# Bias lines drawn in fp32 at the start of an encoder kernel, with their operands loaded on ScalarE's queue

## The chip, the cores and the metric

The kernel runs on one core of one Trainium2 chip. The metric is the device time of one execution in microseconds. Before the change it is 1682.21 us, the median of three runs from 1681.28 to 1682.70 us.

## What is computed

One encoder layer with 1024 channels is run over 1024 sample rows and 256 prompt rows. Every row is normalised (RMS norm with a gain), multiplied with a wide input matrix to queries, keys, values and gates, goes through a windowed attention branch with sinks and a dilated attention branch, is merged by gates, and passes a squared-ReLU MLP. What matters here is the bias table: 32 buckets by 20 heads, looked up by relative position and added to the attention logits.

```python
rel = np.arange(3 * n)[None, :] - n - np.arange(n)[:, None]
bias = bias_table.astype(jnp.float32)[_rel_bucket(rel * dist_scale)]
...
logits = jnp.where(valid[None, :, None, None], s + bias, NEG_INF)
```

## The kernel before

The kernel computes nearly everything on TensorE (PE) with numbers that are split in two parts, hi and lo, each of the type fp32r, and three matmuls for each product. The splitting is done on ScalarE (ACT, the hi part) and VectorE (DVE, the lo part). Each engine works off its instructions strictly in the order in which the program is written; the code around the change fixes that order by hand.

**The opening.** The ten row tiles of 128 rows are loaded by SP's queue (load_x, L684 to L686), with the gain gm (L810) and the value columns of the input matrix (load_v, L688 to L696) between them. For each tile, `square` (L733) takes the row's sum of squares and its root on ACT, `scale` (L740) multiplies by the reciprocal and the gain on DVE and so makes xn, and `turn` (L748) transposes xn on PE (eight 128x128 transposes, L338) and splits the result from PSUM (hi on ACT, L769, lo on DVE, L771). `split_v` (L698) splits the value weights. `values` (L792) then multiplies: 24 matmuls of 128x512 for each tile, L798. Fillers on PE are issued by `warm` (L708): matmuls of the identity by itself, 15 ahead of the first tile, 4 behind the first tile's transposes, 2 behind the second's. The order written out at L831 to L887 is: square, scale and transposes of tile 0, warm(4), square and scale of tile 1, the split of tile 0, transposes of tile 1, warm(2), and then the value matmuls.

**The bias lines.** The bias depends on the relative position alone, so the kernel draws 2048 positions ("lines", NL = 2048) for all 20 heads: a one-hot matrix of 33 rows (32 buckets, and one row for masked positions with -1e30) by 2048 positions, an input made on the host, is multiplied by the table. Before the change this is done in four steps of 512 positions, one in each of the tiles 3 to 6 (`draw`, L722): the table is split into tab_hi and tab_lo on DVE (L861, L862), POOL loads 512 columns of the one-hot rows (`load_hot`, L715, tile hs) and converts them to fp32r (L720, tile hr), PE makes two matmuls (L727), ACT copies 20x512 out of PSUM (L729), and POOL stores them in the DRAM scratch scr_l (L730). From the first pair of column blocks on, `line` (L296) spreads scr_l for the attention.

**Loads and their counters.** SP and ACT each have a hardware queue for loads and stores. The framework gives these transfers eight completion counters, DMAHW0 to DMAHW7, in turn, in the order in which the program writes the transfers, whichever of the two queues they are on. A transfer that takes over a counter is preceded, on the engine that issues it, by a wait until the counter's last user has landed. POOL's transfers have counters of their own (DMASW).

Of the kernel before, what the change touches and what calls it, by code (L numbers as in the profile page):

```python
# [10 lines left out]
F32 = mybir.dt.float32  # L11
F32R = mybir.dt.float32r
AF = mybir.ActivationFunctionType
ALU = mybir.AluOpType

P = 128
D = 1024
# [6 lines left out]
AH = 8  # L24
BH = 4
FF = 4 * D
EPS = 1e-6
NEG = -1e30
BUCKETS, MAXD = 32, 1024
# [68 lines left out]
def encoder_kernel(  # L98
# [5 lines left out]
    nc = tc.nc  # L104
# [15 lines left out]
    const = ctx.enter_context(tc.tile_pool(name="const", bufs=1))  # L120
# [6 lines left out]
    def slot(name, shape=(P, D), dt=F32):  # L127
        return slots.tile(list(shape), dt, name=name, tag="m", bufs=N_M)
# [7 lines left out]
    def bank(tag, name=None):  # L136
        return psum.tile([P, 512], F32, name=name or tag, tag=tag, bufs={"mm": 3, "sc": 2, "pt": 2, "pv": 1}[tag])
# [111 lines left out]
    nc.vector.memset(eps, EPS)  # L249
    bg = const.tile([P, 2 * KC], F32, name="bg")  # L250
    nsink = const.tile([P, AH], F32, name="nsink")
    tab = const.tile([BUCKETS + 1, AH + 3 * BH], F32, name="tab")
    tab_hi, tab_lo = (const.tile([BUCKETS + 1, AH + 3 * BH], F32R, name=x) for x in ("tab_hi", "tab_lo"))

    nm_b = const.tile([P, ROWS], F32, name="nm_b")
    l_b = const.tile([P, ROWS], F32, name="l_b")
# [19 lines left out]
    NH = AH + 3 * BH  # L276
# [16 lines left out]
    NL = sum(x[5] for x in LINES)  # L293
    scr_l = dram.tile([NH, NL], F32, name="scr_l")
# [378 lines left out]
    with ExitStack() as pre:  # L673
        late = pre.enter_context(tc.tile_pool(name="values", bufs=1))

        def own(name, shape, dt=F32, n=1):
            return late.tile(list(shape), dt, name=name, tag=name, bufs=n)
# [6 lines left out]
        def load_x(t):  # L684
            xs[t] = slot("xt")
            nc.sync.dma_start(xs[t], x_rows(t))  # L686
# [11 lines left out]
        def split_v(v, i, eng=nc.vector):  # L698
            if v == 0:
                hi, lo = wslot("vhi", (P, 2, 512), F32R), wslot("vlo", (P, 2, 512), F32R)  # L700
            else:
                hi, lo = own("v2", (P, 2, 384), F32R, 8), own("v2", (P, 2, 384), F32R, 8)
            src = v_raw.pop((v, i))
            nc.scalar.activation(hi, src, AF.Copy)
            eng.tensor_tensor(lo, src, hi.bitcast(F32), op=ALU.subtract)
            v_parts[v, i] = hi, lo

        def warm(n):  # L708
            ps = bank("mm", "warm")
            for _ in range(n):  # L710
                nc.tensor.matmul(ps[:, :P], ident, ident, start=True, stop=True, skip_group_check=True)

        hots = {}

        def load_hot(i):  # L715
            if i < NL // 512:
                hs = own("hs", (P, 512))[: BUCKETS + 1, :]
                nc.gpsimd.dma_start(hs, hot[:, 512 * i : 512 * i + 512])
                hots[i] = own("hr", (P, 512), F32R)[: BUCKETS + 1, :]
                nc.gpsimd.tensor_copy(hots[i], hs)  # L720

        def draw(i):  # L722

            ps = bank("pv", "line")
            hs = hots.pop(i)
            for k, x in enumerate((tab_lo, tab_hi)):
                nc.tensor.matmul(ps[:NH, :], x, hs, start=not k, stop=k == 1)  # L727
            ln = own("vo", (P, 512), n=2)[:NH, :]
            nc.scalar.activation(ln, ps[:NH, :], AF.Copy)  # L729
            nc.gpsimd.dma_start(scr_l[:, 512 * i : 512 * i + 512], ln)  # L730
            load_hot(i + 1)

        def square(t):  # L733
            xn[t] = slot("xn")
            ss = small.tile([P, 1], F32, name="ss")
            nc.scalar.activation(xn[t], xs[t], AF.Square, accum_out=ss)
            sds[t] = small.tile([P, 1], F32, name="sd")
            nc.scalar.activation(sds[t], ss, AF.Sqrt, bias=eps, scale=1.0 / D)

        def scale(t):  # L740
            rs = small.tile([P, 1], F32, name="rs")
            nc.vector.reciprocal(rs, sds.pop(t))
            nc.vector.scalar_tensor_tensor(xn[t], xs.pop(t), rs, gm, op0=ALU.mult, op1=ALU.mult)
# [48 lines left out]
        def values(t, v, ps, ks=range(KC)):  # L792
            n = NV[v]
            for k in ks:
                lh, ll = h_at(k, P * t, P)
                rh, rl = (x[:, k % 2, :] for x in v_parts[v, k // 2])
                for j, (a, b) in enumerate(((lh, rh), (lh, rl), (ll, rh))):
                    nc.tensor.matmul(ps[:, :n], a, b, start=k == 0 and j == 0, stop=k == KC - 1 and j == 2)  # L798

        def evac(t, v, ps):  # L800
            rows = slice(P * t, P * t + P)
            vo = own("vo", (P, 512), n=2)[:, : NV[v]]
            if v == 0:
                nc.vector.tensor_copy(vo, ps)
            else:
                nc.scalar.activation(vo, ps[:, : NV[v]], AF.Copy)
            nc.gpsimd.dma_start(scr_v[rows, 512 * v : 512 * v + NV[v]], vo)
# [5 lines left out]
            load_v(0, i)  # L813
        for t in range(2, 6):
            load_x(t)
        nc.sync.dma_start(tab[:BUCKETS, :], rel_bias)
        nc.sync.dma_start(bg, b_gate[0].rearrange("(k p) -> p k", p=P))
        nc.sync.dma_start(nsink, sink[0].partition_broadcast(P))
        load_v(1, 0)
# [10 lines left out]

        turns = [turn(t) for t in range(NT)]  # L831
        square(0)
        scale(0)
        next(turns[0])
        warm(4)
        square(1)
        scale(1)
        next(turns[0])
        split_v(0, 0)
        next(turns[1])  # L840
        warm(2)
        split_v(0, 1)
        next(turns[1])
        split_v(0, 2, nc.gpsimd)
# [12 lines left out]
        next(turns[1], None)  # L857
        square(4)
        next(turns[2], None)
        nc.vector.memset(tab[BUCKETS:, :], NEG)  # L860
        nc.vector.tensor_copy(tab_hi, tab)  # L861
        nc.vector.tensor_tensor(tab_lo, tab, tab_hi.bitcast(F32), op=ALU.subtract)  # L862
        load_hot(0)
        nc.vector.tensor_scalar(nsink, nsink, -1.0, None, op0=ALU.mult)
        for t in range(2):
            evac(t, 0, pss[t])
# [2 lines left out]
        for t in range(2, NT):  # L869
            if t + 1 < NT:  # L870
                next(turns[t + 1])
                next(turns[t + 1])
            if t + 3 < NT:
                square(t + 3)
            if t + 2 < NT:
                scale(t + 2)
            if t + 1 < NT:
                next(turns[t + 1], None)
            if t < 6:
                split_v(1, t - 2)  # L880
            if t > 7:
                next(b0)
            ps = bank("mm", "v")
            values(t, 0, ps)
            if 3 <= t < 3 + NL // 512:
                draw(t - 3)
            evac(t, 0, ps)  # L887

        def more():
# [14 lines left out]
        for t in (4, 5, 6, 7, 8, 9, 0, 1, 2, 3):  # L904
            ps = bank("mm", "v")
# [6 lines left out]
    if True:  # L912
# [16 lines left out]
        class Rows:  # L929
# [15 lines left out]
            def sum(self, t0, n, ps, other):  # L945
                out, a, b = self.views(t0, n, ps, other)
                nc.vector.scalar_tensor_tensor(out, a, self.scale, b, op0=ALU.mult, op1=ALU.add)
# [401 lines left out]
    if True:  # L1349
# [54 lines left out]
        n = len(order)  # L1404
# [87 lines left out]
        for i, (x, b, c) in enumerate(jobs):  # L1492
            t0, n = BLOCKS[b]
# [15 lines left out]
            ps = bank("mm")  # L1509
# [79 lines left out]
    with ExitStack() as pre:  # L1589
# [20 lines left out]
        for hh in range(2):  # L1610
# [17 lines left out]
            for t in range(NT):  # L1628
                m = parts.pop(t)
                ps = bank("mm")  # L1630
# [391 lines left out]
```

## Time and profile before

| | |
|---|---|
| median of three runs | 1682.21 us |
| the profiled execution's own time | 1681.33 us |
| its span, first to last instruction | 1679.5 us |
| busy PE, DVE, ACT, POOL | 1667.2, 951.4, 718.2, 512.1 us |
| mean granted TensorE clock | 0.999 |

A row of the timeline gives the start in us, the duration in us, the engine, the line, the operation, what is written from what, and in brackets the idle time before it and what ended it. "SPq" and "ACTq" are transfers as the engine issues them. An fp32 matmul that isn't fp32r has two records in the trace (15 fillers have 30). The rows of transfers give the size and the time from the issue to the landing.

### The profile page before, as it was taken

Reading aid. Unit: us, or ns where it says so; the run is one execution under the profiler, and the core shown is the slowest. Engines: PE = TensorE matmul, PEld = TensorE weight load, DVE = VectorE, ACT = ScalarE, POOL = GpSimd, SP = SyncE. Lnnn points to the kernel's source line nnn. Section 1 sums busy time; section 2 is a strip of 40 time slices with the busy share of each in tenths; the row PEclk is TensorE's granted clock in tenths of the full one; section 3 lists DMA queues with packets and bytes.
Section 4 is the critical chain, followed back from the end, with each engine's and each line's share of the span. In section 5 each row is a group of like instructions: output and inputs, shape, how many; then the busy total and the mean of one; then the engine's idle time right before and its main releaser. Section 6 shows DMA issues by size and latency. Waiting matters only on the chain. (4 is left out here: it accounts for less than half of the span.)

```text
span 1679.5 us, 24942 instructions
## 1 busy us (share of the span) xinstructions
PE 1667.2 (99%) x9268; PEld 1414.5 (84%) x9268; DVE 951.4 (57%) x1544; ACT 718.2 (43%) x1485; POOL 512.1 (30%) x404
## 2 busy tenths in 40 slices
PE   9999999999999999999999999999999999999998
PEld 7898888887788888888888888888888888888886
DVE  6732233455563566677278445545556775867665
ACT  6332323356662556654176333333334333333445
POOL 1312222122111463200100556556454250514240
PEclk9999999999999999999999999999999999999999
DMA  7426562567676793845121443443356934733333
GB/s 249 151 58 127 133 133 76 162 192 197 192 198 188 184 262 119 296 133 201 38 88 59 160 156 109 136 160 115 125 190 227 363 105 131 256 102 116 120 119 125
DMA packets 225881, 262.45 MB, mean 156 GB/s; under 512 B 30017, under 2 KB 154737, under 8 KB 225761
## 3 DMA queue, kind: packets, MB, share of 16 engines
q1 hardware_dynamic: 217536, 239.80, 44.8%
q0 software_dynamic: 7936, 20.54, 5.6%
q8 instruction: 73, 1.20, 0.3%
q10 hardware_dynamic: 288, 0.52, 0.1%
q14 instruction: 48, 0.39, 0.1%
HBM read 175.13 MB, written 90.92 MB: 158 GB/s over the span
## 5 line engine op out<-in xcount | busy, mean ns | idle before, releaser
L347 PE MATMUL dn<-dhi,ulo 128*128 128x512 f32 x448 | 174.5, 389 | 0.2
L347 PE MATMUL dn<-dlo,uhi 128*128 128x512 f32 x448 | 174.3, 389 | 0.0
L347 PE MATMUL dn<-dhi,uhi 128*128 128x512 f32 x448 | 174.3, 389 | 0.0
L347 PE MATMUL x<-chi,wlo 128*128 128x512 f32 x424 | 167.0, 394 | 0.1
L347 PE MATMUL x<-clo,whi 128*128 128x512 f32 x424 | 165.7, 391 | 0.1
L347 PE MATMUL x<-chi,whi 128*128 128x512 f32 x424 | 165.1, 389 | 0.0
L314 DVE TENSOR_TENSOR wlo<-ta,whi 128x1024 fp32r<-128x1024 f32 x30 | 55.2, 1841 | 173.8 <-ACT whi L312 173.8
L314 DVE TENSOR_TENSOR wlo<-raw,whi 128x1024 fp32r<-128x1024 f32 x60 | 89.0, 1483 | 98.1 <-ACT whi L312 96.5
L393 POOL TENSOR_TENSOR tb<-raw 128x512 f32<-128x512 f32 x25 | 32.5, 1298 | 366.8 <-DMA raw<-in_w_in_dram 146.5
L347 PEld LDWEIGHTS dn<-dhi,ulo 128*128 128x128 f32 x448 | 84.1, 188 | 18.4 <-PE dn L347 0.5
L347 PEld LDWEIGHTS dn<-dlo,uhi 128*128 128x128 f32 x448 | 84.1, 188 | 17.5
L347 PEld LDWEIGHTS dn<-dhi,uhi 128*128 128x128 f32 x448 | 84.1, 188 | 17.4
L347 PEld LDWEIGHTS x<-chi,whi 128*128 128x128 f32 x424 | 79.6, 188 | 17.0
L347 PEld LDWEIGHTS x<-chi,wlo 128*128 128x128 f32 x424 | 79.8, 188 | 15.7 <-ACT c L1936 0.6
L347 PEld LDWEIGHTS x<-clo,whi 128*128 128x128 f32 x424 | 79.8, 188 | 14.9 <-DVE clo L314 0.4
L1716 POOL TENSOR_TENSOR t<-raw,t 128x1024 f32<-128x1024 f32 x16 | 45.0, 2828 | 154.3 <-DMA raw<-in_w_down_dram 154.3
L186 DVE TENSOR_TENSOR ulo<-uraw,uhi 128x1024 fp32r<-128x1024 f32 x56 | 88.7, 1606 | 3.5 <-ACT uhi L185 3.5
L1865 DVE TENSOR_TENSOR v<-v,dn 128x512 f32<-128x512 f32 x90 | 59.4, 682 | 41.2 <-PE dn L347 36.6
L1965 POOL TENSOR_TENSOR u<-u,u 128x640 f32<-128x640 f32 x16 | 25.1, 1570 | 171.7 <-ACT u L1883 171.7
L186 DVE TENSOR_TENSOR dlo<-raw,dhi 128x1024 fp32r<-128x1024 f32 x32 | 48.6, 1540 | 47.2 <-ACT dhi L185 46.3
L347 PE MATMUL dn<-dhi,up 128*128 128x512 f32 x224 | 73.5, 389 | 0.0
L185 ACT ACTIVATE dhi<-raw 128x1024 fp32r<-128x1024 f32 x32 | 33.5, 1058 | 93.5 <-PE dn L347 93.0
(325 smaller groups left out, 4690.6 us busy)
## 6 DMA issues: line engine op xcount, KB each, us to landing
scr_u<-u SPq DMA_DIRECT2D x112, 320.0 KB, 2.6
uraw<-scr_u SPq DMA_DIRECT2D x56, 512.0 KB, 4.5
raw<-in_w_down_dram SPq DMA_DIRECT2D x36, 512.0 KB, 6.2
raw<-in_w_up_dram SPq DMA_DIRECT2D x32, 512.0 KB, 5.4
raw<-in_w_in_dram SPq DMA_DIRECT2D x25, 512.0 KB, 5.4
sg<-scr_g SPq DMA_DIRECT2D x32, 256.0 KB, 6.3
uraw<-scr_u SPq DMA_DIRECT2D x28, 256.0 KB, 4.3
v<-scr_v SPq DMA_DIRECT2D x96, 64.0 KB, 2.8
```

The source lines that it names most:

```text
L185: nc.scalar.activation(hi, src, AF.Copy)
L186: nc.vector.tensor_tensor(lo, src, hi.bitcast(F32), op=ALU.subtract)
L314: nc.vector.tensor_tensor(lo, src, hi.bitcast(F32), op=ALU.subtract)
L347: nc.tensor.matmul(ps, a, b, start=first and i == 0, stop=last and i == len(seq) - 1, skip_group_check=True)
L393: (nc.vector if vector else nc.gpsimd).tensor_tensor(o, x, y, op=ALU.subtract)
L1716: nc.gpsimd.tensor_tensor(o, a, b, op=ALU.subtract)
L1865: nc.vector.tensor_tensor(v, v, ps, op=ALU.add)
L1965: nc.gpsimd.tensor_tensor(u[S1], u21, u22, op=ALU.add)
```

## The change

The table stays in fp32, and one matmul for each 512 positions takes the place of two. The table is now a 33x224 tile of zeros with the 20 columns of the heads at column 96 (`tab`). A window of 128 columns that begins at 96 - 32j puts the heads at rows 32j to 32j + 19 of the result, so that four matmuls add up into one PSUM bank, 512 positions each, at four places of 32 rows. ACT copies the whole bank (128x512) once, in tile 3, and POOL stores the four places. The table and the one-hot rows (now two tiles of 33x1024, out of the pool of 4 KB slots) are loaded on ACT's queue, and the one-hot rows are used without conversion. `draw(0)` stands in place of warm(4), and draws 1 to 3 in place of warm(2).

```diff
-    tab = const.tile([BUCKETS + 1, AH + 3 * BH], F32, name="tab")
-    tab_hi, tab_lo = (const.tile([BUCKETS + 1, AH + 3 * BH], F32R, name=x) for x in ("tab_hi", "tab_lo"))
...
-        hots = {}
+        pads = NL // 512
+        edge = 32 * (pads - 1)
+        tab = own("tab", (P, edge + P))[: BUCKETS + 1, :]
+        nc.vector.memset(tab, 0.0)
+        nc.vector.memset(tab[BUCKETS:, edge : edge + NH], NEG)
+        nc.scalar.dma_start(tab[:BUCKETS, edge : edge + NH], rel_bias)
+        hots = []
+        drawn = bank("pv", "line")
 
         def load_hot(i):
-            if i < NL // 512:
-                hs = own("hs", (P, 512))[: BUCKETS + 1, :]
-                nc.gpsimd.dma_start(hs, hot[:, 512 * i : 512 * i + 512])
-                hots[i] = own("hr", (P, 512), F32R)[: BUCKETS + 1, :]
-                nc.gpsimd.tensor_copy(hots[i], hs)
-
-        def draw(i):
-
-            ps = bank("pv", "line")
-            hs = hots.pop(i)
-            for k, x in enumerate((tab_lo, tab_hi)):
-                nc.tensor.matmul(ps[:NH, :], x, hs, start=not k, stop=k == 1)
-            ln = own("vo", (P, 512), n=2)[:NH, :]
-            nc.scalar.activation(ln, ps[:NH, :], AF.Copy)
-            nc.gpsimd.dma_start(scr_l[:, 512 * i : 512 * i + 512], ln)
-            load_hot(i + 1)
+            hots.append(slot("hot")[: BUCKETS + 1, :])
+            nc.scalar.dma_start(hots[i], hot[:, D * i : D * i + D])
+
+        def draw(j):
+
+            nc.tensor.matmul(drawn, tab[:, edge - 32 * j : edge - 32 * j + P],
+                             hots[j // 2][:, 512 * (j % 2) : 512 * (j % 2) + 512], start=not j, stop=j == pads - 1)
+
+        def store_lines():
+
+            ln = own("vo", (P, 512), n=2)
+            nc.scalar.activation(ln, drawn, AF.Copy)
+            for j in range(pads):
+                nc.gpsimd.dma_start(scr_l[:, 512 * j : 512 * j + 512], ln[32 * j : 32 * j + NH, :])
...
-        nc.sync.dma_start(tab[:BUCKETS, :], rel_bias)
...
         square(0)
+        load_hot(0)
+        load_hot(1)
         scale(0)
         next(turns[0])
-        warm(4)
+        draw(0)
         square(1)
         scale(1)
         next(turns[0])
         split_v(0, 0)
         next(turns[1])
-        warm(2)
+        for j in (1, 2, 3):
+            draw(j)
...
-        nc.vector.memset(tab[BUCKETS:, :], NEG)
-        nc.vector.tensor_copy(tab_hi, tab)
-        nc.vector.tensor_tensor(tab_lo, tab, tab_hi.bitcast(F32), op=ALU.subtract)
-        load_hot(0)
...
-            if 3 <= t < 3 + NL // 512:
-                draw(t - 3)
+            if t == 3:
+                store_lines()
```

**ScalarE at the start of the program**, before the change, with the counters that each instruction waits for. xt is a tile of the rows as loaded, xn the squares (later the normalised tile), ss and sd the sum of squares and its root.

```order
L736 ACTIVATE xn,ss<-xt 128x1024 [waits DMAHW0_49]
L738 ACTIVATE sd<-ss,eps 128x1 [waits Activation_49]
L736 ACTIVATE xn,ss<-xt 128x1024 [waits DMAHW2_49]
L738 ACTIVATE sd<-ss,eps 128x1 [waits Activation_49]
L769 ACTIVATE hhi<-tr 128x2x128 [waits PE_49]
```

The same place of the changed program:

```order
L716 DMA tab<-in_rel_bias_dram 32x20 [waits DVE_49]
L830 ACT_TABLE_LOAD
L830 ACTIVATE sd<-eps 128x1
L739 ACTIVATE xn,ss<-xt 128x1024 [waits DMAHW0_49]
L741 ACTIVATE sd<-ss,eps 128x1 [waits Activation_49]
L722 DMA hot<-in_hot_dram 33x1024 [waits DMAHW2_49]
L722 DMA hot<-in_hot_dram 33x1024 [waits DMAHW3_49]
L739 ACTIVATE xn,ss<-xt 128x1024
L741 ACTIVATE sd<-ss,eps 128x1 [waits Activation_49]
L772 ACTIVATE hhi<-tr 128x2x128 [waits PE_49]
```

The two loads of one-hot rows now stand between the squares of tile 0 and of tile 1, each with a wait on a counter.

**SP's queue in the changed program**, from the first load to the two loads of row tiles 8 and 9 (xt from in_x_prompt). The counters DMAHW2 and DMAHW3 go, in turn, to gm and row tile 1, to row tiles 4 and 5, to row tiles 6 and 7, and then to the two loads of one-hot rows.

```order
L684 DMA xt<-in_x_sample_dram 128x1024 [waits DMAHW2_49]
L684 DMA xt<-in_x_sample_dram 128x1024 [waits DMAHW3_49]
L819 DMA bg<-in_b_gate_dram 128x16x1 [waits DMAHW4_49]
L820 DMA nsink<-in_attn_sink_dram 128x8 [waits DMAHW5_49]
L693 DMA vraw<-in_w_in_dram 128x2x128 [waits DMAHW6_49]
L694 DMA vraw<-in_w_in_dram 128x2x256 [waits DMAHW7_49]
L693 DMA vraw<-in_w_in_dram 128x2x128 [waits DMAHW0_49]
L694 DMA vraw<-in_w_in_dram 128x2x256 [waits DMAHW1_49]
L684 DMA xt<-in_x_sample_dram 128x1024 [waits DMAHW2_49]
L684 DMA xt<-in_x_sample_dram 128x1024 [waits DMAHW3_49]
```

The first two of these rows are row tiles 4 and 5, the last two are row tiles 6 and 7. What moved on SP's queue is the table's load, which stood ahead of bg's before and has gone to ACT.

**PE at the start of the changed program**, with its waits (line is the PSUM bank of the bias lines, tr that of the transposes, v that of the values):

```order
L709 MATMUL warm<-ident 128x128 x14
L336 MATMUL tr<-ident,xn 128x128 [waits DVE_49]
L336 MATMUL tr<-ident,xn 128x128 x7
L726 MATMUL line<-hot,tab 128x512 [waits DMAHW2_49,DMAHW1_49]
L336 MATMUL tr<-ident,xn 128x128 [waits DVE_49]
L336 MATMUL tr<-ident,xn 128x128 x7
L726 MATMUL line<-hot,tab 128x512
L726 MATMUL line<-hot,tab 128x512 [waits DMAHW3_49]
L726 MATMUL line<-hot,tab 128x512
L801 MATMUL v<-vhi,hhi 128x512 [waits Activation_49]
```

Before, the first `line` row was four fillers and the three others were two fillers; the eight 20x512 matmuls ahead of the transposes of tiles 4 to 7 are gone.

## The prediction

> **What bounds the kernel now.** First the page's totals and then the waits of PE, for the whole span (engine, line, what it waited for, us in total, times, longest).
>
> ```profile
> PE 1667.2 (99%) x9268; PEld 1414.5 (84%) x9268; DVE 951.4 (57%) x1544; ACT 718.2 (43%) x1485; POOL 512.1 (30%) x404
> ...
> PE tr L338 <- DVE xn L743: 1.2, 2, 0.9
> PE sc L1146 <- DVE m L1148: 1.0, 2, 0.7
> PE v L798 <- DVE vlo L705: 0.7, 1, 0.7
> ```
>
> PE is busy 1667.2 of 1679.5 us. Behind the opening the longest of its waits is the 1.0 us of the attention, in two pieces. So PE sets the end, and no later slack can take up a delay of PE in the opening: what the opening loses, the end loses, and a matmul taken out of a dense stretch of PE is won at the end. The question is therefore when PE's dense stretch begins, and how many slots are gone from it. The timeline of the opening, before the change:
>
> ```profile
> 4.79 1.06 ACT L736 ACTIVATE xn<-xt 128x1024 f32<-128x1024 f32 x1 [2.56 <-DMA xt<-in_x_sample_dram]
> 5.97 0.29 ACT L738 ACTIVATE sd<-ss,eps 128x1 f32<-128x1 f32 x1
> 7.87 1.06 ACT L736 ACTIVATE xn<-xt 128x1024 f32<-128x1024 f32 x1 [1.60 <-DMA xt<-in_x_sample_dram]
> ...
> 10.91 1.09 PE L338 MATMUL tr<-ident,xn 128*128 128x128 f32 x8 [0.92 <-DVE xn L743]
> 11.84 0.61 PE L711 MATMUL warm<-ident 128*128 128x128 f32 x4
> 13.37 0.50 PE L798 MATMUL v<-vlo,hhi 128*128 128x512 f32 x1 [0.68 <-DVE vlo L705]
> 13.71 0.40 PE L798 MATMUL v<-vhi,hlo 128*128 128x512 f32 x1
> ...
> 21.20 0.39 PE L798 MATMUL v<-vhi,hlo 128*128 128x512 f32 x1
> ```
>
> ACT squares tile 1 at 7.87 us, when its row tile has landed; the transposes of tile 1 follow at 10.91, 3.04 us later; the value matmuls run without a gap from the third, at 13.71, to the 36th, at 21.20: 33 steps in 7.49 us, 0.227 each. Counted back by two steps, the dense stretch begins at an effective **13.26 us**.
>
> **The loads.** The change puts two loads into ACT's row of instructions, between the squares of tiles 0 and 1, and each waits for a completion counter. What such a wait costs shows on SP's queue. Its issues (start, duration), its waits, and the landing times of single transfers, in the order of their issue at 2.12, 2.60, 3.39 (value columns), 9.42 (table), 20.43 and 20.90 (row tiles 6 and 7, the two of the row with x2):
>
> ```profile
> 2.12 0.43 SPq L693 DMA_DIRECT2D vraw<-in_w_in_dram  x1
> 2.60 0.75 SPq L693 DMA_DIRECT2D vraw<-in_w_in_dram  x1
> 3.39 0.62 SPq L693 DMA_DIRECT2D vraw<-in_w_in_dram  x1
> 4.79 3.40 SPq L686 DMA_DIRECT2D xt<-in_x_sample_dram  x4
> 9.42 0.34 SPq L816 DMA_DIRECT2D tab<-in_rel_bias_dram  x1
> 10.76 0.39 SPq L817 DMA_DIRECT2D bg<-in_b_gate_dram  x1
> 12.12 6.25 SPq L818 DMA_DIRECT2D nsink<-in_attn_sink_dram  x1
> ...
> 20.43 0.94 SPq L686 DMA_DIRECT2D xt<-in_x_sample_dram  x2
> ...
> SPq L816 <- DMA vraw<-in_w_in_dram: 1.2, 1, 1.2
> ...
> vraw<-in_w_in_dram SPq DMA_DIRECT2D x1, 512.0 KB, 7.3
> vraw<-in_w_in_dram SPq DMA_DIRECT2D x1, 512.0 KB, 8.2
> vraw<-in_w_in_dram SPq DMA_DIRECT2D x1, 512.0 KB, 8.7
> tab<-in_rel_bias_dram SPq DMA_DIRECT2D x1, 2.5 KB, 9.8
> xt<-in_x_sample_dram SPq DMA_DIRECT2D x1, 512.0 KB, 5.7
> xt<-in_x_sample_dram SPq DMA_DIRECT2D x1, 512.0 KB, 6.5
> ```
>
> The reader is to see three pairs of numbers. The table is issued at 9.42, and the first value columns land at 2.12 + 7.3 = 9.42; bg is issued at 10.76, and the second ones land at 2.60 + 8.2 = 10.80; nsink at 12.12, and the third ones land at 3.39 + 8.7 = 12.09. None of them uses the other's data: each transfer waits for the one eight places ahead of it, whose counter it takes. In the changed program the order of writing is table, row tile 0, gm, row tile 1, four value columns, row tiles 2 to 5, bg, nsink, four value parts, **row tiles 6 and 7**, four value parts, row tiles 8 and 9, and then the two loads of one-hot rows. Eight back from these stand row tiles 6 and 7. They land at 20.43 + 5.7 = 26.1 and 20.90 + 6.5 = 27.4 us. The loads were written at the end of the list but stand early in ACT's order, and all of ACT is queued behind them: the square of tile 1, the splits of tiles 0 and 1 and of the value weights. For those DVE waits, and for DVE the transposes of tile 1 and all value matmuls.
>
> Does SP's queue keep its times? The same bytes stand ahead of row tiles 6 and 7 as before, less the table's 2.5 KB; nsink's issue lasts 6.25 us, and I keep that, as it starts and ends among the same transfers. If it fell away, row tile 7 would still wait for row tile 5, the last of the four issued from 4.79; the table, next behind it, landed at 9.42 + 9.8 = 19.2, so the issue could come 1.7 us before 20.90. POOL's stores and one-hot loads also leave this stretch, for some tenths at most. I take 27.4, and keep 25.4 as an end.
>
> **From there to the dense stretch.** The rows that are still needed:
>
> ```profile
> 1675.62 0.35 ACTq L1835 DMA_DIRECT2D out_dram<-v  x1
> ...
> hs<-in_hot_dram POOLq DMA_DIRECT2D x1, 66.0 KB, 3.0
> ...
> 1.36 6.36 PE L711 MATMUL warm<-ident 128*128 128x128 f32 x30 [1.36 <-POOL ident masks.py:199]
> ...
> 6.85 0.54 PE L711 MATMUL warm<-ident 128*128 128x128 f32 x2
> 7.07 0.43 PE L711 MATMUL warm<-ident 128*128 128x128 f32 x2
> 7.22 0.39 PE L711 MATMUL warm<-ident 128*128 128x128 f32 x2
> 7.33 0.39 PE L711 MATMUL warm<-ident 128*128 128x128 f32 x2
> ```
>
> ACT issues a transfer in 0.35 us, so the second load is out at 27.8, and the square of tile 1 starts at about **27.9** in place of 7.87. Its transposes could start 3.04 us later, at 30.95. The first load goes out at 26.1; one-hot rows of half its size took 3.0 us on POOL's queue beside the stream of row tiles, so it lands near 29.1, and draw(0) starts then.
>
> Two prices are not shown directly. One is PE's rate after 20 us of idleness. At the program's start the fillers' records stand 0.21 us apart (6.85, 7.07) and from about 7.1 on 0.11 apart (7.22, 7.33): PE ran at half its rate for 5.7 us after its first matmul, though the windows' clock column says 1.00 throughout. I take the same 5.7 us after draw(0), to 34.8; the ends are no slow time at all, and slow until the draws are over. [...]
>
> The other is an fp32 matmul of 512 columns. A filler, fp32 with 128 columns, takes two records of 0.107 to 0.11 us at the full rate, so four times the columns take 8 x 0.11 = 0.9 us (1.8 slow). From the other side, the nearest row is the fp32r value matmul of the same width, 0.23; half way, two passes would be 0.45. I take 0.9, as the filler is the same kind of instruction. So draw(0) runs from 29.1 to 30.9, hidden in the wait for xn; the eight transposes at 0.21 take 30.95 to 32.65; draw 1 to 34.5, draw 2 to 35.5, draw 3 to **36.4**. Everything else the value matmuls need is early by then: the lo part that PE waited for at 13.37 comes 20 us later, at 33.4. The dense stretch begins at 36.4 in place of 13.26: **+23.1 us**.
>
> **What is won.** The four draws in the tiles are gone. One of them, from the last value matmul to the transposes:
>
> ```profile
> 51.61 0.39 PE L798 MATMUL v<-vhi,hlo 128*128 128x512 f32 x1
> 51.93 0.41 PE L727 MATMUL line<-hr,tab_lo 33*20 33x512 f32 x1
> 52.18 0.39 PE L727 MATMUL line<-hr,tab_hi 33*20 33x512 f32 x1
> 52.49 0.33 PE L338 MATMUL tr<-ident,xn 128*128 128x128 f32 x1
> ...
> 40.00:60.00 20.00, 20.00 (x96) 15.06 (x95) 19.52 (x42) 9.79 (x24) 5.77 (x11) 1.00 0.20 65
> ```
>
> From 51.61 to 52.49 are 0.88 us, of which 0.23 are the value matmul's own; 4 x 0.65 = **-2.6 us**. In the window from 40 to 60 us (columns: us, then PE, PEld, DVE, ACT, POOL busy) DVE is busy 19.52 of 20 us, so a shorter tile could make DVE the bound; I cost that at nothing, because PE now starts 3.1 us later behind DVE than before (23.1 against 20.0), which is more than the 2.6. If that cover fails, the 2.6 us are not won.
>
> The rest costs nothing: the casts and one-hot loads of POOL, and the table's split on DVE, go from engines that nobody waits for there; the new memset of 33x224 is done before DVE's first use at 6.3; ACT's table load starts a little later but was over 2.56 us before the first square; the single copy of 128x512 takes the place of the first 20x512 one, with the same columns, and three others are gone; POOL's four stores come in one place, well ahead of the spreading of the lines in the first pairs.
>
> **Sum:** 23.1 - 2.6 = +20.5 us on the profiled execution's 1681.33 (its span of 1679.5 and 1.8 around it) gives 1701.8; the median of the runs is 0.9 higher than that execution. I predict **1702.2 us**.
>
> **The rivals.**
>
> The loads do not hold ACT up: the counters' last users were others, or the wait sits in the queue and not on the engine. For it speaks that the trace shows such waits on SP only, which does nothing else. Then square 1 stays at 7.87, the one-hot rows go out at 6.3 and land about 3.0 us later, at 9.3; draw(0) fits before 10.91 at the full rate; draws 1 to 3 run from 11.8 to 14.5, and the dense stretch begins 1.2 late: 1.2 - 2.6 = -1.4, **1680 us**, which is not slower than before. It decides from the point where the first one-hot rows land by 10 us. Chance 6%. [...]
>
> As before, but the one-hot rows queue behind the row tiles as the table did, which took 9.8 us: they land at 16.1, draw(0) is done at 17.0, the transposes at 17.9, the other draws at 20.7, with some slow clock 22: +8.7 - 2.6, **1688 us**. Against it stands that POOL's one-hot load took 3.0 us beside the same stream. 3%.
>
> The stall is there, but PE comes up sooner. [...] Together 22%.
>
> The stall is there, and the gain of 2.6 is eaten by DVE, or PE stays slow through the draws (1.7 more): **1704 to 1705 us**. 15%.
>
> My forecast itself, 1701.4 to 1703.5: 54%.
>
> **How the numbers follow.** The stall's cases hold 91%. Their ends are 25.4 in place of 27.4 with short draws (1698) and a late PE with no gain (1706). The range 1698 to 1706 leaves out the two cases without the stall, 9%, and some tails. A measurement of this kernel can tell about 0.2%, or 3.4 us, from no change. Slower by more than that: 91% and the 3% of late rows, so 94%; within it: 5%; faster: 1%.
>
> **What would show it.** In the changed profile: ACT idle from 6.3 to 27.9, ended by the landing of row tile 7; ACT's two transfers issued near 26.1 and 27.4; the transposes of tile 1 near 31; the value matmuls from 36.4 on, 0.23 apart; draw records 0.9 apart while PE is slow, 0.45 later; the transposes of tiles 4 to 7 one step of 0.23 behind the value matmuls. I am wrong if ACT's square of tile 1 starts near 8, or if row tiles 6 and 7 land well ahead of 25.

## The result, and the profile after

The changed kernel takes 1710.13 us, the median of five runs (1708.82 to 1710.94), beside 1682.09 us for the kernel before (five runs): ratio 1.0167, with a 95% interval from 1.0156 to 1.0179. That is +28.0 us; +20.5 had been forecast, to 1702.2 us. The direction, and the stall from which it comes, are as predicted; the time lies above the range of 1698 to 1706.

The page of the profiled execution after (1708.82 us):

```profile
span 1707.0 us, 24898 instructions
PE 1673.2 (98%) x9256; PEld 1417.6 (83%) x9256; DVE 954.4 (56%) x1543; ACT 716.2 (42%) x1482; POOL 511.2 (30%) x396
```

PE still sets the end. The span is 27.5 us longer, PE's busy time only 6.0. The waits of PE, over the whole span (what it waited for, us in total, times, longest):

```profile
PE line L726 <- DMA hot<-in_hot_dram: 23.7, 1, 23.7
PE tr L336 <- DVE xn L746: 0.2, 1, 0.2
```

One wait holds nearly all of the new idle time, and it is draw(0)'s own wait for its one-hot rows, not the wait for xn that the prediction named. The timeline of ACT in the opening (start, duration, what was done, idle time before it):

```profile
26.72 1.68 ACTq L722 DMA_DIRECT2D hot<-in_hot_dram  x2
28.45 1.06 ACT L739 ACTIVATE xn<-xt 128x1024 f32<-128x1024 f32 x1 [22.18 <-DMA xt<-in_x_sample_dram]
```

The square of tile 1 starts at 28.45, not at 7.87. The trace names the landing of a row tile as what ended the 22.18 us of idleness; tile 1 had been there for some 20 us (before the change its square starts at 7.87), so it is the counter of row tile 6 or 7 that ACT's loads waited for: these tiles went out at 20.15 and 20.66 us, the two loads at 26.72 and 28.09. ACT's last instruction ahead of the loads (L741) ended at 6.26, and from there to 26.72 ACT did nothing, so the wait stood on ACT itself.

The timeline of PE from there on:

```profile
7.95 1.09 PE L336 MATMUL tr<-ident,xn 128*128 128x128 f32 x8 [0.23 <-DVE xn L746]
32.75 2.04 PE L726 MATMUL line<-hot,tab 33*128 33x512 f32 x2 [23.70 <-DMA hot<-in_hot_dram]
34.72 1.97 PE L336 MATMUL tr<-ident,xn 128*128 128x128 f32 x8
36.62 5.49 PE L726 MATMUL line<-hot,tab 33*128 33x512 f32 x6
42.03 0.79 PE L801 MATMUL v<-vhi,hhi 128*128 128x512 f32 x1
42.62 0.63 PE L801 MATMUL v<-vlo,hhi 128*128 128x512 f32 x1
...
44.73 0.39 PE L801 MATMUL v<-vhi,hhi 128*128 128x512 f32 x1
44.95 0.39 PE L801 MATMUL v<-vlo,hhi 128*128 128x512 f32 x1
...
51.55 1.03 PE L336 MATMUL tr<-ident,xn 128*128 128x128 f32 x8
...
67.86 1.03 PE L336 MATMUL tr<-ident,xn 128*128 128x128 f32 x8
...
87.48 1.07 PE L336 MATMUL tr<-ident,xn 128*128 128x128 f32 x8
```

The reader is to see the steps between rows. Each of the three later draws takes 1.8 us (5.41 for three, up to 42.03), the first six value matmuls stand about 0.43 apart, and from the seventh, at 44.73, they stand 0.23 apart. Counted back by six steps of 0.227 the dense stretch begins at an effective 43.37 us: +30.1 against 13.26. The same three transposes before the change, those of tile 2 and those behind the first and the fourth of the old draws:

```profile
21.43 1.03 PE L338 MATMUL tr<-ident,xn 128*128 128x128 f32 x8
...
38.37 1.10 PE L338 MATMUL tr<-ident,xn 128*128 128x128 f32 x8
...
59.55 1.09 PE L338 MATMUL tr<-ident,xn 128*128 128x128 f32 x8
```

The first agree with the +30.1: 51.55 against 21.43. The second now begin at 67.86, 29.5 later, and the third at 87.48, 27.9 later. So 2.2 us are back by there, of 2.6 forecast. (The last two are the transposes of tiles 5 and 8: a draw at the end of tile t stands ahead of those of tile t + 2, and the "tiles 4 to 7" ahead of this section are one too low.) At the end the spans are 27.5 us apart.

The windows of the changed kernel (stretch, length, busy PE, PEld, DVE, ACT, POOL, then the granted clock, DMA share, GB/s):

```profile
26.00:28.00 2.00, 0.00 (x0) 0.00 (x0) 0.00 (x0) 0.00 (x0) 0.00 (x0) 0.50 1.10 344
28.00:30.00 2.00, 0.00 (x0) 0.00 (x0) 0.05 (x1) 1.52 (x4) 0.00 (x0) 0.50 1.06 404
42.00:44.00 2.00, 2.00 (x6) 1.58 (x6) 1.96 (x3) 1.05 (x3) 0.00 (x0) 0.50 0.00 0
46.00:48.00 2.00, 2.00 (x11) 1.65 (x10) 0.00 (x0) 0.00 (x0) 0.00 (x0) 1.00 0.00 0
```

PE was busy without a gap from 32.75, yet its clock stayed at 0.50 until about 44.6: 11.9 us, where the forecast had 5.7. And the one-hot rows were issued while the DMA engines were full (1.10, 1.06).

So three questions were left: is the stall ACT's wait for the counters, or PE's wait for the one-hot rows? Why did the rows take 6.0 us to land (26.72 to 32.75), not 3.0? Why did the clock stay low for so long?

### The profile page after: what moved, and what is told of

Same layout as the page of the kernel before. It is cut to its first block, busy times and chain, and to the rows that moved or that the text cites. A ratio compares the mean times of both kernels' runs of the same rounds, so it can differ in the third digit from the quotient of the medians.

```text
span 1707.0 us, 24898 instructions
## 1 busy us (share of the span) xinstructions
PE 1673.2 (98%) x9256; PEld 1417.6 (83%) x9256; DVE 954.4 (56%) x1543; ACT 716.2 (42%) x1482; POOL 511.2 (30%) x396
## 4 chain that ended last, share of the span: by engine, by line
PE 94%; DMA 2%; DVE 2%; ACT 1%; SPq 1%; issue 0%; ACTq 0%; DVEq 0%
PE dn L345 22%; PE x L345 19%; PE mm L192 14%; PE z L345 9%; PE v L801 6%; PE y L345 5%; PE mm L345 5%; PE sc L345 3%; PE pv L345 3%; PE pv L1189 2%; PE pt L1173 1%; PE sc L539 1%; PE pv L584 1%; PE pt L571 1%; PE sc L1147 1%; PE tr L336 1%
## 5 line engine op out<-in xcount | busy, mean ns | idle before, releaser
L1866 DVE TENSOR_TENSOR v<-v,dn 128x512 f32<-128x512 f32 x90 | 59.4, 681 | 38.9 <-PE dn L345 34.5
L345 PE MATMUL z<-chi,wlo 128*128 128x512 f32 x184 | 72.0, 391 | 0.0
```

The costliest lines, as they stand in the source:

```text
L345: nc.tensor.matmul(ps, a, b, start=first and i == 0, stop=last and i == len(seq) - 1, skip_group_check=True)
L1866: nc.vector.tensor_tensor(v, v, ps, op=ALU.add)
```

## The experiments

The first four ran on one chip, where the kernel before took 1681.02 us (9 runs). From chip to chip the kernel before takes 1680.81 to 1682.47 us, so differences are given to the kernel before on the same chip; there the changed kernel has +28.0.

### The hold alone

The kernel before, with two unread loads of the one-hot rows on ACT's queue behind the first square.

```diff
         square(0)
+        for i in range(2):
+            nc.scalar.dma_start(slot("hot")[: BUCKETS + 1, :], hot[:, D * i : D * i + D])
         scale(0)
```

> The kernel of before with nothing but the two loads of one-hot rows on ACT's queue, at the place where the change has them; nobody reads them. Theory (the hold on ACT is the larger part by itself): ACT squares tile 1 near 28.4, the transposes of tile 1 come at 31.4 and not at 34.7, the clock is slow for the first value matmuls: 1701 to 1706 us. Rival (PE's wait for the one-hot rows is what costs): no more than 1685 us.

One run, 1701.07 us: **+20.0 us** with no draw moved and nobody waiting for the data. Its timeline:

```profile
26.78 1.64 ACTq L834 DMA_DIRECT2D hot<-in_hot_dram  x2
28.47 1.06 ACT L736 ACTIVATE xn<-xt 128x1024 f32<-128x1024 f32 x1 [22.32 <-DMA xt<-in_x_sample_dram]
...
31.51 1.97 PE L338 MATMUL tr<-ident,xn 128*128 128x128 f32 x8 [21.58 <-DVE xn L743]
```

The transposes of tile 1 start at 31.51, 3.04 us behind the square, as forecast from the rows of before. In the trace the value matmuls run at full rate from about 35.1, 3.6 us after the transposes began, where the changed kernel needed 11.9 us from draw(0).

### The same loads with no earlier user of their counters

```diff
+        load_hot(0)
+        load_hot(1)
         load_x(0)
...
         square(0)
-        load_hot(0)
-        load_hot(1)
         scale(0)
```

> The changed kernel with one thing moved: both loads of one-hot rows are written ahead of all row tiles, so their counters have no earlier user. Theory (ACT is held by the counters of row tiles 6 and 7): the hold goes, ACT squares tile 1 near 8 us, the dense stretch of PE begins 1 to 2 us late for the draws' width, and the four old draws give 2.6 us back: 1680 to 1682 us. Rival (the loads on ACT's queue or the draws themselves are slow, whatever the counters): most of the 28 us stays, above 1700 us.

1688.08 us (5 runs, 1685.60 to 1688.64), ratio 1.0038 (1.0024 to 1.0052) to before. The hold is gone: the same loads on the same queue, written first, leave +7.1 us in place of +28.0. But 1680 to 1682 had been expected. The timeline of its opening:

```profile
9.18 1.06 ACT L739 ACTIVATE xn<-xt 128x1024 f32<-128x1024 f32 x1 [2.98 <-DMA xt<-in_x_sample_dram]
...
9.31 1.12 PE L726 MATMUL line<-hot,tab 33*128 33x512 f32 x2
12.23 1.09 PE L336 MATMUL tr<-ident,xn 128*128 128x128 f32 x8 [1.80 <-DVE xn L746]
13.25 4.47 PE L726 MATMUL line<-hot,tab 33*128 33x512 f32 x6
```

The square of tile 1 is 1.3 us late, with 264 KB more in flight beside its row tile, and draws 1 to 3 take 4.4 us where the full rate would need 2.7. A window of this kernel shows the clock:

```profile
14.00:18.00 4.00, 4.00 (x6) 1.24 (x5) 4.00 (x7) 3.97 (x9) 2.24 (x1) 0.54 1.03 410
```

PE is busy all through it, and its clock falls to half. One draw, 1.80 us of idleness and the transposes stand ahead of it.

### Fillers in the stall

100 fillers ahead of draw(0), to bring the clock up before it.

```diff
         next(turns[0])
+        warm(100)
         draw(0)
```

> The changed kernel with 100 fillers on PE ahead of draw(0), about 22 us at the full rate, which end before the one-hot rows land at 32.7. Theory (part of the 28 us is PE at half rate after its idleness): PE is at the full rate when the rows land; draw(0) 0.9, transposes 0.9, three draws 2.7, so the value matmuls begin near 37.3 and run at 0.227 at once, 6 us earlier than the changed kernel's effective 43.4: about 1703 us. Rival (the draws are slow in themselves, 1.8 us each): they stay slow, and only the value matmuls gain, about 1707 us.

One run, 1712.49 us, where 1703 or 1707 had been expected. The timeline:

```profile
8.97 22.50 PE L709 MATMUL warm<-ident 128*128 128x128 f32 x200
...
34.54 2.04 PE L726 MATMUL line<-hot,tab 33*128 33x512 f32 x2 [3.07 <-DMA xt<-in_x_prompt_dram]
```

The fillers ended at 31.5, and the rows landed later than in the changed kernel (at 34.5). The granted clock fell to half at 34.2, in the gap of 3.07 us, so draw(0) took 2.04 us: the fillers ended too early for it. What the run shows of the draws is that the clock stayed at half through 13.3 us of PE work without a gap, up to 47.9, 4.0 us after the first value matmul.

### Draws over all 128 rows

The table and the one-hot tiles are padded with zeros to 128 rows, so that each draw reads 128 rows in place of 33; its length is the same.

```diff
-        tab = own("tab", (P, edge + P))[: BUCKETS + 1, :]
+        tab = own("tab", (P, edge + P))
...
-            hots.append(slot("hot")[: BUCKETS + 1, :])
-            nc.scalar.dma_start(hots[i], hot[:, D * i : D * i + D])
+            hots.append(slot("hot"))
+            nc.gpsimd.memset(hots[i], 0.0)
+            nc.scalar.dma_start(hots[i][: BUCKETS + 1, :], hot[:, D * i : D * i + D])
```

> The changed kernel with table and one-hot rows filled up with zeros to 128 rows, so that a draw uses all rows of PE's array. Theory A (matmuls over 33 of 128 rows do not count as the activity that raises the clock): the clock rises 5 to 6 us after draw(0), near 38.5, two of the draws run at the full rate: 1704.5 to 1706 us. Theory B (the rise depends on time or on the kind of matmul, not on its rows): the clock rises near 44.6 as in the changed kernel, 1708 to 1710 us.

One run, 1705.35 us: +24.3 where the changed kernel has +28.0. Its timeline of PE, then its windows:

```profile
32.87 2.05 PE L727 MATMUL line<-hot,tab 128*128 128x512 f32 x2 [23.78 <-DMA hot<-in_hot_dram]
34.71 1.70 PE L336 MATMUL tr<-ident,xn 128*128 128x128 f32 x8
36.25 2.74 PE L727 MATMUL line<-hot,tab 128*128 128x512 f32 x6
38.42 0.80 PE L802 MATMUL v<-vhi,hhi 128*128 128x512 f32 x1
39.06 0.40 PE L802 MATMUL v<-vlo,hhi 128*128 128x512 f32 x1
```

```profile
34.00:36.00 2.00, 2.00 (x9) 1.38 (x8) 0.00 (x0) 0.19 (x1) 0.00 (x0) 0.50 0.00 0
36.00:38.00 2.00, 2.00 (x8) 1.04 (x8) 1.42 (x4) 2.00 (x6) 0.00 (x0) 0.99 0.00 0
```

Everything up to the transposes of tile 1 starts at the same times as in the changed kernel (32.87 against 32.75, 34.71 against 34.72). Then the clock rises near 36.0, about 3.2 us after draw(0) began and sooner than the 38.5 expected, and the second value matmul follows the start of the later draws by 2.8 us (36.25 to 39.06), where the changed kernel needs 6.0 (36.62 to 42.62). The transposes of tile 2 come 4.5 us earlier (47.04). From draw(0) on PE's work differs in nothing but the rows of the operands: with the draws over 128 rows the clock rose 3.2 us after draw(0) began, with those over 33 rows 11.9 us after it.

### Draws in tile 3

Loads and hold as in the changed kernel; all four draws at the end of tile 3, so that PE does not wait for the rows in the opening.

```diff
-        draw(0)
...
-        for j in (1, 2, 3):
-            draw(j)
...
             if t == 3:
+                for j in range(pads):
+                    draw(j)
                 store_lines()
```

> The changed kernel with all four draws in tile 3, where the lines are copied out: the hold on ACT stays, PE waits for no one-hot rows in the opening. Theory: the transposes of tile 1 come at about 31.5 as with the two loads alone, the clock is up some 3.5 us later, the draws cost 3.6 us in the dense stretch or, when the clock falls under them, up to 3 us more, and the old ones are gone: 1700 to 1705 us. Rival (PE's wait for one-hot rows is the larger part): near 1685 us.

One run, 1705.65 us (before on its chip: 1680.81 us, 17 runs). Transposes of tile 1 at 30.52, full rate from about 35.5, 5.0 us later: the rise after full-row work took 3.2 (draws over 128 rows), 3.6 (the hold alone) and 5.0 us in three runs. The draws' row, then the windows behind it, and two short ones in which the clock falls and rises again:

```profile
58.63 3.70 PE L726 MATMUL line<-hot,tab 33*128 33x512 f32 x8
```

```profile
62.00:64.00 2.00, 2.00 (x11) 1.65 (x11) 0.68 (x2) 1.50 (x4) 0.75 (x2) 0.71 0.00 0
64.00:66.00 2.00, 2.00 (x6) 1.58 (x5) 1.97 (x4) 0.87 (x3) 1.29 (x3) 0.50 0.36 80
```

```profile
62.75:63.00 0.25, 0.25 (x4) 0.25 (x3) 0.04 (x1) 0.25 (x2) 0.00 (x0) 0.71 0.00 0
...
66.25:66.50 0.25, 0.25 (x3) 0.21 (x2) 0.25 (x2) 0.25 (x2) 0.11 (x1) 0.96 0.00 0
```

Two readings: at the full rate a draw takes 3.70 / 4 = 0.92 us, so the 0.9 of the forecast was right. And the clock fell to 0.50 behind 3.6 us of draws with PE busy before, in and after them; the four draws cost their own time and this spell.

### A quieter queue for the rows

Row tiles 8 and 9 go to POOL's queue, later; two loads of 4 KB keep their places in SP's order, so that the counters stay as they are.

```diff
-        load_x(8)
-        load_x(9)
+        for i in range(2):
+            nc.sync.dma_start(own(f"pad{i}", (P, AH)), sink[0].partition_broadcast(P))
...
         split_v(0, 2, nc.gpsimd)
+        for t in (8, 9):
+            xs[t] = slot("xt")
+            nc.gpsimd.dma_start(xs[t], x_rows(t))
```

> The changed kernel without the stream of row tiles 8 and 9 beside the one-hot loads: at their place on SP's queue stand two loads of 4 KB, and both row tiles come later on POOL's queue. Theory (one-hot rows landed 6 us after their issue because they shared the engines with that stream): draw(0) starts within about 3 us of the first load's issue, near 29, the transposes of tile 1 near 31, 3 to 4 us ahead of the changed kernel: 1704 to 1706 us. Rival (the load's own shape, 33 rows of 4 KB on ACT's queue, is slow): again 6 us from issue to draw(0).

One run, 1707.61 us (same chip as the last). The first load went out at 24.54, two microseconds earlier, and draw(0) began at 30.22, 5.7 us behind the issue, as the rival (the load's own shape) had it and not within 3 us. But the queue had not become quiet: the last value weights took 6 to 7 us beside it, and the DMA share was 1.02 and 1.10 in the two windows from 24 to 28 us. So the run leaves the question open.

### The rows on POOL's queue from the start, with 128 and with 33 rows

Here nothing on ACT is held: its square of tile 1 starts at 8.10 us (128 rows) and 9.36 (33 rows). Draws 0 and 1 follow the transposes of tile 0, draws 2 and 3 those of tile 1. The first kernel has the zero padding of above, the second reads 33 rows and needs no zeroing.

```diff
-            hots.append(slot("hot")[: BUCKETS + 1, :])
-            nc.scalar.dma_start(hots[i], hot[:, D * i : D * i + D])
+            hots.append(slot("hot"))
+            nc.gpsimd.memset(hots[i], 0.0)
+            nc.gpsimd.dma_start(hots[i][: BUCKETS + 1, :], hot[:, D * i : D * i + D])
...
+        load_hot(0)
+        load_hot(1)
         load_x(0)
...
         square(0)
-        load_hot(0)
-        load_hot(1)
         scale(0)
...
         draw(0)
+        draw(1)
...
-        for j in (1, 2, 3):
+        for j in (2, 3):
```

> The changed kernel with the one-hot rows loaded on POOL's queue at the start, whose transfers share no counter with SP and ACT, filled up with zeros to 128 rows, and draws 0 and 1 behind the first tile's transposes, 2 and 3 behind the second's. Theory (hold on ACT, late rows and a clock that 33-row draws do not keep up are all that costs): all three are gone, the dense stretch of PE begins 1 to 2 us late, the four old draws give 2.6 us back: 1679.5 to 1681.5 us, level with the kernel of before or just ahead. Rival (fp32 draws in the opening cost in some further way): above 1684 us.

> The same without the zeros: draws over 33 rows. Theory A (33-row matmuls do not count as activity): the clock falls to half during the draws though PE has work, and stays there for some 3.5 us of the value matmuls: 2 to 5 us more than with 128 rows, 1682 to 1686 us. Theory B (rows do not matter): the same time as with 128 rows, within 1 us.

With 128 rows: 1681.14 us (11 runs), ratio 1.0000 (0.9991 to 1.0008). With 33: 1686.05 us (7 runs), ratio 1.0030 (1.0019 to 1.0041). Both are without the hold: +0.3 and +5.2 us in place of +28.0. The 128-row form is level with before, with a clock of 1.00 through its opening. The kernel with 33 rows, timeline and one window:

```profile
9.31 1.98 PE L726 MATMUL line<-hot,tab 33*128 33x512 f32 x4
12.41 1.09 PE L336 MATMUL tr<-ident,xn 128*128 128x128 f32 x8 [1.12 <-DVE xn L746]
13.44 3.41 PE L726 MATMUL line<-hot,tab 33*128 33x512 f32 x4
```

```profile
14.00:16.00 2.00, 2.00 (x4) 0.67 (x2) 2.00 (x3) 2.00 (x6) 0.06 (x1) 0.50 1.02 407
```

The pair is not clean: without the zeroing the loads went out earlier (1.30 against 2.13), the square of tile 1 came later (9.36 against 8.10), and PE stood idle for 1.12 us between the pairs of draws.

### That pair made clean, and 64 rows

Zeroing and loads as with 128 rows; the draws alone read 33 rows (on another chip, before 1681.17 us, 13 runs), or tiles of 64 rows are used.

```diff
-            nc.tensor.matmul(drawn, tab[:, edge - 32 * j : edge - 32 * j + P],
-                             hots[j // 2][:, 512 * (j % 2) : 512 * (j % 2) + 512], start=not j, stop=j == pads - 1)
+            nc.tensor.matmul(drawn, tab[: BUCKETS + 1, edge - 32 * j : edge - 32 * j + P],
+                             hots[j // 2][: BUCKETS + 1, 512 * (j % 2) : 512 * (j % 2) + 512], start=not j, stop=j == pads - 1)
```

> As the run with the zero-padded rows on POOL's queue (128 rows, 1681.14 us), zeroing and loads as there, so that everything lands as there; the draws alone read 33 of the 128 rows. It parts two causes of the spell of half clock in the run with 33 rows on POOL's queue (1686.05 us), where row tile 1 landed later as well and PE stood idle for 1.12 us between two pairs of draws. Theory A (33-row draws don't keep the clock up, whatever stands between them): the clock falls behind the draws for about 4 us here too, total 1682.5 to 1685 us. Rival B (the idle 1.12 us beside the draws made it fall): the clock stays at 1.00 and the total is 1680.5 to 1681.8 us, as with 64 and 128 rows.

> As the run with the zero-padded rows on POOL's queue, with 64 rows of table and one-hot in place of 128 (33 used, 31 zeros). Theory A (a matmul over few of the 128 rows holds the clock less): with half of the rows the clock either stays at 1.00 (total about 1681 us, as with 128 rows) or falls as with 33 (total 1684 to 1686 us); which of them says where between 33 and 128 rows the border lies. Rival B (the draws of 33 rows fell for another reason, the later row tile 1): 64 rows fall like 33, and 128 rows held only by luck: 1684 to 1686 us.

With 33 rows: 1681.14 us (10 runs, 1680.46 to 1685.86), ratio 1.0005 (0.9996 to 1.0015). The theory as I had put it missed. PE of the profiled execution:

```profile
9.43 1.98 PE L727 MATMUL line<-hot,tab 33*128 33x512 f32 x4
11.35 1.09 PE L336 MATMUL tr<-ident,xn 128*128 128x128 f32 x8
12.37 1.98 PE L727 MATMUL line<-hot,tab 33*128 33x512 f32 x4
```

Two pairs of draws, 1.9 us each, with full-row transposes between them and no idle time, kept the full rate (clock 1.00 in all windows from 10 to 26 us). So in this run 33-row work did not push the clock down. It held through two spells of 1.9 us without full-row work; with 3.1 us of draws and idle time together (9.31 to 12.41), and a pair of draws behind the next transposes, it did not hold in the run above, but fell at 13.85. Two of the ten runs took 1683.72 and 1685.86 us at mean clocks of 0.997 and 0.996; whether the clock fell behind the draws in them is not shown, and the kernel before has single runs of 1684.89 and 1685.69 us too (0.998). With 64 rows, one run of 1680.43 us (before 1682.47, one run): level, but as 33 rows hold there too, that run tells nothing of where the border lies.

### What the landing depends on

Four loads of 66 KB in place of two of 132 KB, on POOL's queue at the start; and two loads of 132 KB on POOL's queue in tile 3, where the DMA engines are nearly idle (share 0.00 from 36 to 42 us), with the draws (33 rows) and the storing in tile 5. Before on this chip: 1682.47 us, one run. The edit of the first, and then that of the second, without the draws that fall away in the opening:

```diff
+            for c in (0, 512):
+                nc.gpsimd.dma_start(hots[i][: BUCKETS + 1, c : c + 512], hot[:, D * i + c : D * i + c + 512])
```

```diff
-            nc.scalar.dma_start(hots[i], hot[:, D * i : D * i + D])
+            nc.gpsimd.dma_start(hots[i], hot[:, D * i : D * i + D])
...
-            if t == 3:
+            if t == 5:
+                for j in range(pads):
+                    draw(j)
                 store_lines()
             evac(t, 0, ps)
+            if t == 3:
+                load_hot(0)
+                load_hot(1)
```

> The two one-hot loads on POOL's queue at the start are cut into four loads of half the bytes, 33 rows by 512 (66 KB each); the rest is as in the run with the zero-padded rows on POOL's queue (draws of 128 rows after each tile's transposes, 1681.14 us). It asks why the 132 KB loads landed 6.3 and 7.3 us after their issue there, and 6.0 us in the changed kernel, while the row of 66 KB in the kernel before had 3.0 us. Theory A (they share the DMA engines with the row tiles, whose stream is full in the opening): the 66 KB loads land 5 to 7 us after issue as well, and the total stays at 1680 to 1683 us. Rival B (the bytes of the load decide): they land about 3 us after issue, with the same total.

> The two one-hot loads (132 KB each) go to POOL's queue in tile 3, where the windows show the DMA engines nearly idle, and the draws (33 rows) to tile 5, with the row's storing behind them. Theory A (in the opening the loads landed late because the row tiles' stream was full): here they land 2 to 3.5 us after issue. Rival B (size and shape of the load, not the stream): about 6 us again. The total is a by-product: the hold on ScalarE is gone, the draws cost about 3.6 us in the dense stretch and a spell of lower clock behind them, and the four old draws' 2.6 us fall away: 1682 to 1687 us.

The transfers' rows (size, us from issue to landing), of the 66 KB loads at the start:

```profile
hot<-in_hot_dram POOLq DMA_DIRECT2D x4, 66.0 KB, 6.1
```

of the 132 KB loads at the start, and of those in tile 3:

```profile
hot<-in_hot_dram POOLq DMA_DIRECT2D x2, 132.0 KB, 6.8
```

```profile
hot<-in_hot_dram POOLq DMA_DIRECT2D x2, 132.0 KB, 3.1
```

Half the bytes gained 0.7 us; idle DMA engines gained 3.7. In these runs the stream decided the landing far more than the size. The totals, one run each, are 1680.78 and 1682.61 us. The second holds a surprise. Its draws and the windows around them:

```profile
50.32 3.70 PE L726 MATMUL line<-hot,tab 33*128 33x512 f32 x8
```

```profile
52.00:54.00 2.00, 2.00 (x6) 0.62 (x4) 1.90 (x6) 0.00 (x0) 0.00 (x0) 1.00 0.00 0
54.00:56.00 2.00, 2.00 (x14) 1.82 (x14) 2.00 (x4) 1.95 (x6) 1.06 (x3) 1.00 0.00 0
```

The same 3.6 us of 33-row draws, in the same dense surroundings as in tile 3 above, and this time the clock stays at 1.00.

## Why the prediction was wrong by its size

**PE sets the end, and its delay in the opening goes to the end: right.** +30.1 at the start of the dense stretch, less what the old draws gave back, is the +27.5 of the span.

**The two loads hold ACT until row tiles 6 and 7 have landed: right, and shown.** The square of tile 1 came at 28.45 (forecast 27.9). The loads alone make the kernel before 20.0 us longer; with the same loads written first (square at 9.18), or on POOL's queue (8.10 and 9.36), it was not held.

**"One-hot rows of half its size took 3.0 us on POOL's queue beside the stream of row tiles, so it lands near 29.1": this step failed**, and with it "draw(0) runs from 29.1 to 30.9, hidden in the wait for xn". The rows landed at 32.75, 6.0 us after the issue. The row of 3.0 us was from a load issued at 16.8, just as the stream of row tiles ran dry (DMA share 0.58 from 18 to 20 us, in the windows of before), and it does not hold for a load issued amid a stream of 1.10. Size was no excuse either way: 66 KB took 6.1 us in the full opening, 132 KB took 3.1 with the engines idle. So xn of tile 1 was ready at 31.4, but its transposes stood behind draw(0) until 34.72 in place of 30.95: **+3.8 us**, of which 0.5 is the later square and 3.3 the rows.

**"I take the same 5.7 us after draw(0), to 34.8": this step failed as well.** The half rate lasted 11.9 us. The three later draws took 5.41 us in place of 3.75 (+1.7), the six slow value matmuls 2.70 in place of 1.36 (+1.3), the transposes 1.9 in place of 1.7 (+0.2): **+3.2 us**. What the runs show in its place: where PE had nothing but full-row work after the stall, the clock rose 3.2, 3.6 and 5.0 us after its start (32.87 to 36.05, 31.51 to 35.09, 30.52 to 35.55); with 33-row draws among it, 11.9 us after draw(0) in the changed kernel. The table gives the times in us at which the granted clock fell to 0.50 and rose again. They are worked out from windows of 0.25 us like the two short ones above: a mean of 0.71 from 62.75 to 63.00 puts the fall at 62.86.

| run | falls at | rises at | difference, us | divided by 3.413 us |
|---|---|---|---|---|
| changed kernel | 13.96 | 44.68 | 30.72 | 9 |
| the hold alone | 14.61 | 35.09 | 20.48 | 6 |
| loads first | 14.32 | 21.14 | 6.83 | 2 |
| fillers in the stall | 34.21 | 47.86 | 13.65 | 4 |
| draws over 128 rows | 12.16 | 36.05 | 23.89 | 7 |
| draws in tile 3, the stall | 11.66 | 35.55 | 23.89 | 7 |
| the same, behind the draws | 62.86 | 66.27 | 3.41 | 1 |
| quieter queue | 13.15 | 43.87 | 30.72 | 9 |
| POOL's queue, 33 rows | 13.85 | 20.68 | 6.83 | 2 |

All nine differences are whole multiples of 3.413 us (30.72 / 9), to within 0.01 us. Why they are, and what sets the place of a fall or a rise in a run, is not shown. In the changed kernel PE had no gap from 32.75 on, and yet the clock stayed at 0.50 through draw(0), 1.9 us of transposes and 5.4 us of 33-row draws; it rose at 44.68, 2.65 us into the value matmuls. With the fillers (34.54 to 47.86) and with the quieter queue (30.22 to 43.87) 13.3 and 13.7 us of PE work without a gap, 7.4 us of each 33-row draws, passed before the rise. With the draws over 128 rows it came 3.2 us after draw(0) began. So in these traces a busy PE was not enough where most of its work was 33-row draws. Why the delay was 3.2 us in one run and 5.0 in another is not shown.

With 3.8 and 3.2 the dense stretch moves from 36.4 to 43.4, where it is. The rival in which PE comes up sooner had the second term the wrong way round: a half rate shorter than 5.7 us after the stall shows only where no 33-row draws stood there (3.2 to 5.0 us), and here it lasted 11.9. The rival with the draws wholly at half rate (1704 to 1705) had half of the second term. The rival of late rows had the first term's cause, but without the stall; none had both.

**A draw takes 0.9 us at the full rate: right** (0.92 in tiles 3 and 5). **-2.6 us for the old draws: about right** as far as tile 8, where 2.2 were back. Without the stall it did not reach the end: with the 128-row draws on POOL's queue the transposes of tile 8 come 1.6 us earlier than before (57.98 against 59.55), and the totals are level. Where those 1.6 us go was not followed.

Two slips change little. The last step of the forecast's sum does not add up, as 1701.8 and 0.9 make 1702.7 and not 1702.2. And row tile 0 has the first counter and the table the second, not the other way round, which moves nothing eight places on.

What stays open: why the same 3.6 us of draws lowered the clock in tile 3 and not in tile 5 of another run, 8 us earlier. In tile 3 it fell at 62.86, 0.6 us after the transposes behind the draws had begun; in the other run it stayed at 1.00 in all windows from 36 to 92 us. How many rows between 33 and 128 would have brought the clock up in the stall also stays open.

## What to carry to other kernels

The two loads on ACT's queue stood in ACT's own order of instructions: everything behind them waited, the next square until 28.45 us, and the loads alone cost the kernel before 20.0 us. So for a load on a compute engine's queue look up, in the order in which the program is written, which transfer used its counter last, and read off when that one lands. For a landing time, take a row from the same load on the DMA engines, not the row of the same size (132 KB took 6.0 us amid the stream and 3.1 with the engines idle). And don't count on thin matmuls (here 33 of 128 rows) to bring TensorE's clock up, nor always to keep it up: in the changed kernel it stayed at 0.50 for 11.9 us, 7.4 of them such draws, where draws padded to 128 rows had it up after 3.2, and in tile 3 it fell behind 3.6 us of them.

## What had not been expected of the hardware

PE's records were without a gap while its granted clock was 0.50: 11.9 us of it in the changed kernel, with 33-row draws making up 7.4 us of them, and the clock fell from 1.00 behind 3.6 us of such draws in tile 3. The same matmuls padded with zeros to 128 rows took the same time (two draws 1.98 us, with 33 as with 128 rows), and with them in the stall the transposes of tile 2 came 4.5 us earlier (47.04 against 51.55). In all eight traces in which the granted clock fell and rose again, the time between is a whole multiple of 3.413 us. Amid the full stream of the opening the loads of 132 KB landed 5.7 to 7.3 us after their issue, on ACT's and on POOL's queue alike, and those of 66 KB 6.1 us after it; with the DMA engines idle 132 KB landed in 3.1 us.
